# Hybrid decoder step: first loads and PSUM banks of the head rearranged, a tile for the extra tokens' values, decay rows spread by GpSimd

## Chip, cores and metric

The kernel runs on one core of a Trainium2 chip. The metric is the device time of one execution in microseconds; three runs of a kernel give a median. One further execution is recorded by the hardware profiler, and its trace is what the rows below come from.

## What is computed

One layer of a decoder over 2048 prompt tokens, 16 meta tokens in front of them, and 8 x 4 tokens of running requests ("extra tokens" are the 32 + 16). All read one input projection of the normalised stream (width 1024) and go through two groups of heads: four mLSTM heads, evaluated in chunks of 128 tokens, and a sliding-window attention. Both are gated, joined by one output projection, and normalised again. The mLSTM part, cut to what the change touches:

```python
b = jnp.cumsum(log_f, axis=1)                       # L tokens of a chunk, per head
dmat = b[:, :, None, :] - b[:, None, :, :] + log_i[:, None, :, :]     # causal, else -inf
inter = b + m[:, None, :]
m_t = jnp.maximum(inter, jnp.max(dmat, axis=2))     # running maximum
w = jnp.exp(dmat - m_t[:, :, None, :])
s_inter = jnp.exp(inter - m_t)
qk = einsum(q, k) * w
num = einsum(qk, v) + einsum(q, c) * s_inter[..., None]
w_state = jnp.exp(b_last[:, None, :] - b + log_i - m_new[:, None, :])
c_new = decay[..., None, None] * c + einsum(w_state, k, v)
```

The carried state starts from the meta tokens' chunk, so the first chunk of prompt tokens needs the meta tokens' gates, keys and values first.

## The kernel before

**Stages.** Prompt tokens go in 16 blocks of 128, a block being a chunk of the mLSTM part. A head prepares the weights: each projection's 1024 x 512 fp32 block is loaded in four parts (`load`), its maximum is taken, and it is split into two fp16 parts (`prep`, L271 on ScalarE and L274 on VectorE). Block 0 is projected with the fp32 weights as they arrive (L415), the later blocks and the extra tokens with the split ones (`proj`, L296 to L299; `proj_e`, L305 and L306). The first phase then runs through the chunks: four projections each (q, k, v, o), gates, the mLSTM steps, and the normalisation of a block two ahead (`norm_x`), with single steps of the extra tokens' work and of the later weights between. The second phase does the attention and output projections. The head lasts to 109.4 us here, the first phase to about 545 us.

**Order.** Instructions are placed on each engine's queue by a scheduler which works from the written order and its own model of times; each engine then takes its queue in order. The first loads are chained (`first`) so that SP issues them one behind the other. Rows of one chunk can stand among those of another.

**Tiles.** PSUM has four kinds of tile: `pj` (2 banks, projections), `pt` (3), `px` (1, extra tokens) and `po` (2). `xs` (two buffers) takes the token blocks as loaded: block 0 `x0`, the extra tokens `xe`, block 1 `x1`. `all_max` spreads a column's maximum to all partitions with a matmul of ones (L135) into a `pt` tile.

**A chunk's decay rows.** `m_rows` transposes the gate columns (L740, L741), scans them along the tokens, and leaves in partitions 0, 32, 64 and 96 one row for each head: `r2` (L748, L749) and `M` (L750). `m_weights` spreads the four rows of `M` to all 128 partitions by one fp32 matmul for each head with a selector `sel` (L759), which fills a `pt` tile `Mb`; from it come `ws` (L769), the weights `wt` (L773 and an exponential), and the inter-chunk factors `SI` (L775). `m_T` multiplies the queries by `SI` on GpSimd (L783, L784), `m_S` makes the weighted scores `At` (L794, L796), and `m_num` uses both (L807, L808). The extra tokens' `M5` is spread the same way (L656).

**Extra tokens.** `xe` is normalised, split and transposed to `ET`; its gates `ge` are a `proj_e` with the split gate weights, and its values `ve` lie in `vaug[1]`, the tile that odd chunks take for theirs (L428).

## Time and profile before

| | |
|---|---|
| time, median of 3 runs | 1077.33 us (1075.49 to 1078.78) |
| profiled execution, its own time | 1080.81 us |
| its span, first to last instruction | 1079.0 us |
| TensorE busy | 1035.4 us, 96% of the span |
| VectorE / ScalarE / GpSimd busy | 730.5 / 442.6 / 254.0 us |
| mean granted TensorE clock | 0.984 |
| moved by DMA | 161.83 MB, 150 GB/s |

Busy times are sums over an engine's instructions. A wait is the idle time in front of an instruction, put down to the event that ended it. Start times in the timelines count from the first instruction; matmuls overlap, so what one costs the queue is read from one start to the next.

### The profile page before, as it was taken

To read this page: it belongs to the slowest core of one execution; us is meant where nothing else is said; L and a number is where in the kernel's file an instruction comes from. 1 tells how busy PE (TensorE), PEld (TensorE's weight loads), DVE (VectorE), ACT (ScalarE), POOL (GpSimd) and SP (SyncE) were. 2 spreads that over 40 slices of the span, in tenths; PEclk is the share of its full clock that TensorE was granted. 3 is DMA by queue.
4 is the path that set the end of the run, shared out by engine and by line. 5 is a ranking of instruction groups with operands and counts; after the bars stand their busy time and mean duration, and the time that the engine had idled before them with its cause. 6 is when DMAs were issued, how large, how long until landed. Compare 5 with 4: busy or idle time off the path is not lost.

```text
span 1079.0 us, 17626 instructions
## 1 busy us (share of the span) xinstructions
PE 1035.4 (96%) x6391; PEld 573.5 (53%) x6391; DVE 730.5 (68%) x2057; ACT 442.6 (41%) x1112; POOL 254.0 (24%) x270
## 2 busy tenths in 40 slices
PE   6979998999999998998999999999999999999996
PEld 3435565655555554555564554555555555555553
DVE  5769666776867796877546686566666566666674
ACT  5646332244444445462234343433343433343430
POOL 2112231321120001113011141333322333322322
PEclk9998999999999998999999999999999999999998
DMA  9756447345785686655686455546445645545452
GB/s 323 202 141 164 110 120 173 97 126 145 232 235 143 190 239 168 208 132 145 232 265 112 79 131 127 137 119 126 102 123 125 132 115 131 110 110 131 113 122 63
DMA packets 245809, 161.83 MB, mean 150 GB/s; under 512 B 207945, under 2 KB 220953, under 8 KB 244409
## 3 DMA queue, kind: packets, MB, share of 16 engines
q1 hardware_dynamic: 245722, 160.70, 57.3%
q8 instruction: 50, 0.82, 0.3%
q14 instruction: 37, 0.30, 0.1%
HBM read 68.22 MB, written 43.58 MB: 104 GB/s over the span
## 4 chain that ended last, share of the span: by engine, by line
PE 65%; DMA 12%; DVE 11%; issue 5%; ACT 4%; POOL 1%; SPq 1%; DVEq 0%; ACTq 0%; POOLq 0%
PE pj L1341 15%; PE pj L299 13%; PE pj L296 12%; PE pj L297 12%; PE pt L1261 3%; DMA xT<-hl 2%; PE po L1314 2%; DMA ea<-in_dram 2%; DMA stg<-hl 1%; DMA kT<-kh 1%; DVE xs L380 1%; DMA wd_o<-w_o 1%; PE px L725 1%; ACT hl L323 1%; DMA da<-e_d 1%
## 5 line engine op out<-in xcount | busy, mean ns | idle before, releaser
L296 PEld LDWEIGHTS <-xT 128*128 128x128 f16 x992 | 98.0, 99 | 103.9 <-issue 7.5
L299 PEld LDWEIGHTS <-xT 128*128 128x128 f16 x992 | 97.0, 98 | 98.3 <-issue 2.9
L297 PEld LDWEIGHTS <-xT 128*128 128x128 f16 x992 | 98.0, 99 | 94.8 <-issue 4.3
L1341 PEld LDWEIGHTS <-EE 128*128 128x128 f16 x720 | 70.8, 98 | 80.3 <-issue 2.2
L1341 PE MATMUL pj<-w_o,EE 128*128 128x512 f16 x360 | 83.7, 384 | 0.0
L1341 PE MATMUL pj<-wr_o,EE 128*128 128x512 f16 x360 | 82.3, 379 | 0.0
L1268 ACT ACTIVATE SI<-SI,nb 128x272 f32<-128x272 f32 (+1 forms) x64 | 32.4, 507 | 66.1 <-DVE nb L1265 66.0
L325 POOL TENSOR_TENSOR lns<-lns,mhalf 128x1 f32<-128x1 f32 (+1 forms) x16 | 20.1, 1256 | 136.9 <-ACT lns L324 123.9
L296 PE MATMUL pj<-w_q,xT 128*128 128x512 f16 x120 | 46.4, 387 | 4.8 <-DMA xT<-hl 4.8
L1274 POOL TENSOR_TENSOR mhl<-SI,mhl 128x32 f16<-128x32 f32 x32 | 13.7, 430 | 157.3 <-ACT mhl L1273 157.3
L783 POOL TENSOR_TENSOR qs<-qT 128x512 f32<-128x512 f16 x16 | 23.2, 1453 | 113.5 <-DMA qT<-qh 50.1
L1268 ACT ACTIVATE g<-g,nb 128x272 f32<-128x272 f32 (+1 forms) x64 | 32.1, 503 | 42.7 <-DVE nb L1265 42.7
L296 PE MATMUL pj<-wr_z,xT 128*128 128x512 f16 x128 | 49.3, 385 | 0.0
L297 PE MATMUL pj<-wr_z,xT 128*128 128x512 f16 x128 | 49.2, 384 | 0.0
L296 PE MATMUL pj<-wr_az,xT 128*128 128x512 f16 x128 | 48.5, 379 | 0.0
L296 PE MATMUL pj<-wr_aq,xT 128*128 128x512 f16 x128 | 48.5, 379 | 0.0
L297 PE MATMUL pj<-wr_aq,xT 128*128 128x512 f16 x128 | 48.5, 379 | 0.0
L297 PE MATMUL pj<-wr_az,xT 128*128 128x512 f16 x128 | 48.5, 379 | 0.0
L296 PE MATMUL pj<-w_o,xT 128*128 128x512 f16 x120 | 47.3, 394 | 0.0
L297 PE MATMUL pj<-w_o,xT 128*128 128x512 f16 x120 | 47.1, 393 | 0.0
L1171 POOL TENSOR_TENSOR xs<-xs,gb 128x1024 f32<-128x1024 f32 (+1 forms) x16 | 42.8, 2675 | 15.4 <-DMA stg<-hl 9.3
L296 PE MATMUL pj<-w_v,xT 128*128 128x512 f16 x120 | 46.4, 386 | 0.0
(459 smaller groups left out, 2506.1 us busy)
## 6 DMA issues: line engine op xcount, KB each, us to landing
stg<-in_dram SPq DMA_DIRECT2D x28, 512.0 KB
xs<-in_dram SPq DMA_DIRECT2D x16, 512.0 KB
h_d<-xs SPq DMA_DIRECT2D x16, 512.0 KB
xT_d<-xT SPq DMA_DIRECT2D x16, 512.0 KB
xs<-h_d SPq DMA_DIRECT2D x16, 512.0 KB
xT<-xT_d SPq DMA_DIRECT2D x16, 512.0 KB
out_dram<-xs SPq DMA_DIRECT2D x15, 512.0 KB
hn_d<-g SPq DMA_DIRECT2D x16, 258.0 KB
```

The source lines that it names most:

```text
L296: T.matmul(ps, xT[:, k, :], w.t[:, k, 0, :n], start=(k == 0), stop=False)
L297: T.matmul(ps, xT[:, k, :], w.t[:, k, 1, :n], start=False, stop=False)
L299: T.matmul(ps, xT[:, KT + k, :], w.t[:, k, 0, :n], start=False, stop=(k == KT - 1))
L323: A.activation(junk[:, D:2 * D], x, AF.Square, bias=nmu, accum_out=ss)
L325: G.tensor_tensor(rs, ve, mhalf[:rows, 0:1], op=ALU.pow)
L783: G.tensor_tensor(c.qs, c.qT[:, 0], c.qT[:, 1], op=ALU.add)
L1171: G.tensor_tensor(z, z, lg[:rows], op=ALU.mult)
L1261: T.matmul(ps[:, lo:], c.qT[:, h], kTs[:, 2 * (h // 4) + x, lo:], start=(x == 0), stop=(x == 1))
L1268: A.activation(p[:, i, lo:], p[:, i, lo:], AF.Exp, bias=nb[:, h:h + 1], accum_out=sums[:, h:h + 1])
L1274: G.tensor_tensor(m[:, 1], p[:, :, 2 * P:], m[:, 0], op=ALU.subtract)
L1314: T.matmul(pso[:, h], l, r, start=False, stop=(i == len(last) - 1), skip_group_check=True)
L1341: T.matmul(ps, c.yT[:, a, :], w[:, k, t, :], start=(first and j == 0), stop=(last and j == len(mm) - 1))
```

## The change

There are five edits. The selector matmuls are replaced by GpSimd `partition_broadcast` instructions into an SBUF tile `Mb` (in `m_rows`, so that they are written right behind `M`) and, for `M5`, straight into `Mb5`; `sel` and its memsets go; the GpSimd library that is loaded is another one. The extra tokens' gates are computed in fp32 from eight transposes of `xe` and the unsplit gate weights, and that part of the code with its scans stands ahead of block 0's split. The gate weights, their bias and the constants are loaded ahead of w_k, and block 1 ahead of w_v. Before the chunks run, `all_max` and the first gates take `po` tiles. `ve` is a tile of the arena.

```diff
     def all_max(a, m):
         n = m.shape[1]
-        ps = pt([P, n, P])
+        ps = (pt if Order.running else po)([P, n, P])
...
-    G.load_library(library_config.standard)
+    G.load_library(library_config.all_libraries[10])
...
     first(xe, x_e)
-    stk = stage(512, "w")
-    load(stk, w_a[1])
-    bA = [bias_tile(0, 512, first), bias_tile(512, 512, first)]
     tg = cst.tile([P, KT, 8], F32, name="tg")
     first(tg, w_g)
     bg = cst.tile([P, 8], F32, name="bg")
     first(bg, b_in[0:1, 2560:2568].partition_broadcast(P))
+    first(cs[:, P:], consts[:, P:])
+    stk = stage(512, "w")
+    load(stk, w_a[1])
+    bA = [bias_tile(0, 512, first), bias_tile(512, 512, first)]
...
-    sel = cst.tile([P, H, P], F32, name="sel")
-    G.memset(sel, 0.0)
-    for h in range(H):
-        G.memset(sel[32 * h:32 * h + 1, h], 1.0)
...
         if n == 0:
-            ps = pt([P, 8])
+            ps = po([P, 8])
             proj32(ps, lambda k: tg[:, k])
...
-    ve = vaug[1][:NE]
+    ve = ea.take(H * 129).rearrange("p (h d) -> p h d", d=129)[:NE]
+    G.memset(ve[:, :, 128:129], 1.0)
...
     scale_qk(0)
+    x1 = work("xs", [P, D])
+    first(x1, x_p[P:2 * P, :])
     stv = stage(512)
     load(stv, w_a[2])
...
     dmat(ET, EE[:, 0])
-    first(cs[:, P:], consts[:, P:])
+    xef = work("kw", [P, 512])[:, 0:8 * NE].rearrange("p (k t) -> p k t", t=NE)
+    ps = pt([P, 8, NE])
+    for j in range(8):
+        T.transpose(ps[:, j], xe[:, j * P:(j + 1) * P], ident[:NE, :NE])
+    A.activation(xef, ps, AF.Copy)
+    ps = pt([P, 8])
+    for k in range(KT):
+        T.matmul(ps[:NE], xef[:, k], tg[:, k], start=(k == 0), stop=(k == KT - 1))
+    V.tensor_tensor(ge, ps[:NE], bg[:NE], op=ALU.add)
     log_sigmoid_rows(ge, NE, 1)
...
-    last = proj_e(ge, ET, wg, 8, bg, t1, ps=pt)
...
         Mb5 = ea.take(160).rearrange("p (h b s) -> p h b s", h=H, s=5)
-        ps = pt([P, H, 40])
         for h in range(H):
-            T.matmul(ps[:, h], sel[:, h], M5, start=True, stop=True)
-        A.activation(Mb5.rearrange("p h b s -> p (h b s)"), ps.rearrange("p h t -> p (h t)"), AF.Copy)
+            G.partition_broadcast(Mb5[:, h].rearrange("p b s -> p (b s)"), M5[32 * h:32 * h + 1], channels=P)
...
         V.scalar_tensor_tensor(M, r2[:, 1], carry.m, b, op0=ALU.subtract, op1=ALU.subtract)
-        c.r2, c.M = r2, M
+        Mb = work("Mb", [P, H, P])
+        for h in range(H):
+            G.partition_broadcast(Mb[:, h], M[32 * h:32 * h + 1], channels=P)
+        c.r2, c.Mb = r2, Mb
...
-        Mb = pt([P, H, P])
-        for h in range(H):
-            T.matmul(Mb[:, h], sel[:, h], c.M, start=True, stop=True)
+        Mb = c.Mb
...
     extra = jobs()
+    Order.running = True
```

The block from `xT0 = work(...)` to `a_proj(0, 1, stk)`, with block 0's split, its q and k projections and the splits of the gate weights and of w_k, is the same text and now stands behind the extra tokens' scans (behind `V.tensor_copy(tok, ...)`).

The scheduler orders all queues anew. Three places, with the new kernel's own line numbers in its rows. First SP in the head: `stg` are the staging tiles of w_q and then w_v, `stage` those of w_k and w_o, `xs` the token blocks, `EE` the extra tokens' split. Before:

```order
L114 DMA tg<-in_dram 128x64
L114 DMA bg<-in_dram 128x8
L114 DMA stage<-in_dram 128x1024 x4
L114 DMA bias<-in_dram 128x512
L101 DMA h_d_149<-xs 128x1024
L101 DMA_TRANSPOSE xT<-hl 128x16x128
L101 DMA_TRANSPOSE EE<-EE 128x8x128
L114 DMA stg<-in_dram 128x1024 x4
L114 DMA bias<-in_dram 128x512
L114 DMA cs<-in_dram 128x752
L114 DMA xs<-in_dram 128x1024
```

Now:

```order
L115 DMA cs<-in_dram 128x752
L115 DMA stage<-in_dram 128x1024 x4
L115 DMA bias<-in_dram 128x512 x2
L115 DMA stage<-in_dram 128x1024 x4
L115 DMA bias<-in_dram 128x512
L102 DMA ea<-in_dram 128x8
L102 DMA h_d_144<-xs 128x1024
L102 DMA_TRANSPOSE xT<-hl 128x16x128
L115 DMA xs<-in_dram 128x1024
L102 DMA_TRANSPOSE EE<-EE 128x8x128
L115 DMA stg<-in_dram 128x1024 x4
L115 DMA bias<-in_dram 128x512
```

The load of block 1 (`xs`, 128x1024) stood behind the loads of w_v, their bias and the constants, and now stands right behind the transpose of block 0.

Second, GpSimd where the chunks begin: L325 (now L324) is the `pow` of a block's normalisation, L783 and L784 (now L789 and L790) the two query operations, L716 (now L721) a step of the extra tokens, ISA the broadcasts. Before:

```order
L1027 MEMSET EE 128x1024
L783 TENSOR_TENSOR qs<-qT 128x512
L325 TENSOR_TENSOR lns<-lns,mhalf 128x1 x3
L673 MEMSET da 128x288
L674 MEMSET da 32x1
L784 TENSOR_TENSOR qs<-qs,SI 128x512
L783 TENSOR_TENSOR qs<-qT 128x512
L716 TENSOR_TENSOR da<-ea,cs 32x1024
```

Now:

```order
L324 TENSOR_TENSOR lns<-lns,mhalf 128x1
L789 TENSOR_TENSOR qs<-qT 128x512
L324 TENSOR_TENSOR lns<-lns,mhalf 128x1 x2
L678 MEMSET da 128x288
L679 MEMSET da 32x1
L662 ISA ea<-ea 128x40 x4
L758 ISA Mb<-rM 128x128 x4
L790 TENSOR_TENSOR qs<-qs,SI 128x512
L721 TENSOR_TENSOR da<-ea,cs 32x1024
L789 TENSOR_TENSOR qs<-qT 128x512
L324 TENSOR_TENSOR lns<-lns,mhalf 128x1
L758 ISA Mb<-rM 128x128 x4
```

A chunk's four broadcasts stand behind a `pow` and ahead of the product with `SI`; block 1's `pow` now comes ahead of the first query addition.

Third, VectorE around chunk 0's rows: `r` and `rM` are `r2` and `M` (L749, L750; now L754, L755), `w_o` the split of w_o, `xs` and `hl` block 3's normalisation and split, `vaug` and `px` the values of the extra tokens and of chunk 1. Before:

```order
L274 SCALAR_TENSOR_TENSOR w_o<-stage,cols,w_o 128x2x512
L749 SCALAR_TENSOR_TENSOR r_712<-fi,cols,rb 128x128
L750 SCALAR_TENSOR_TENSOR rM<-r_712,cols,rb 128x128
L274 SCALAR_TENSOR_TENSOR w_o<-stage,cols,w_o 128x2x512 x3
L379 SCALAR_TENSOR_TENSOR xs<-xs,lns,gb 128x1024
L309 TENSOR_TENSOR g<-g,bias 48x512
L380 SCALAR_TENSOR_TENSOR xs<-xs,lns,gb 128x1024
L315 SCALAR_TENSOR_TENSOR vaug_124<-px,cols,g 48x4x128
L769 TENSOR_TENSOR ws<-am,pt 128x4
L773 SCALAR_TENSOR_TENSOR wt<-pt,am,cs 128x128 x4
```

Now:

```order
L600 TENSOR_TENSOR ea<-ea 128x40
L602 COPY ea<-ea 128x32
L395 SCALAR_TENSOR_TENSOR hl<-xs,cols,hl 128x1024
L308 TENSOR_TENSOR g<-g,bias 48x512
L752 SCALAR_TENSOR_TENSOR rb<-ones,fi 128x128
L753 SCALAR_TENSOR_TENSOR r_708<-fi,cols 128x128
L603 TENSOR_TENSOR ea<-ea 128x32
L665 TENSOR_TENSOR ea<-ea 128x32 x4
L314 SCALAR_TENSOR_TENSOR ea<-px,cols,g 48x4x128
L754 SCALAR_TENSOR_TENSOR r_708<-fi,cols,rb 128x128
L427 SCALAR_TENSOR_TENSOR vaug_119<-pj,cols,bias 128x4x128
L755 SCALAR_TENSOR_TENSOR rM<-r_708,cols,rb 128x128
```

The split of w_o, the passes over block 3 and the extra tokens' values, which followed `M`, now stand ahead of it, and so does chunk 1's evacuation (L427), which came well behind `M` before.

## Rows read from the trace of the kernel before

**Rows 1.** Busy times by stage: stretch, length, each engine (instructions), clock, DMA share, GB/s.

```profile
0.00:109.40 109.40, 90.68 (x367) 45.18 (x368) 82.62 (x219) 63.63 (x114) 20.27 (x31) 0.95 0.72 207
109.40:545.00 435.60, 423.67 (x2623) 245.81 (x2622) 311.03 (x896) 179.65 (x405) 75.95 (x63) 0.98 0.61 171
545.00:1079.00 534.00, 521.03 (x3404) 282.49 (x3401) 336.88 (x944) 199.37 (x593) 157.81 (x177) 0.99 0.52 121
```

**Rows 2.** Timeline of TensorE, block 1: start, length, engine, line, operation, tiles [idle before].

```profile
64.47 0.61 PE L296 MATMUL pj<-w_q,xT 128*128 128x512 f16 x1 [4.84 <-DMA xT<-hl]
...
67.43 0.38 PE L297 MATMUL pj<-w_q,xT 128*128 128x512 f16 x1
```

**Rows 3.** Waits of TensorE over the span: who, for whom, total us, times, longest.

```profile
PE pt L740 <- DVE Gf L481: 4.0, 2, 3.3
...
PE px L305 <- ACT w_v L271: 2.7, 1, 2.7
```

**Rows 4.** Timeline of TensorE, chunk 0 (first two rows) and a later chunk.

```profile
92.53 0.98 PE L656 MATMUL pt<-ea,sel 128*128 128x40 f32 x8
93.34 0.39 PE L299 MATMUL pj<-w_v,xT 128*128 128x512 f16 x1
...
434.54 1.05 PE L759 MATMUL pt<-rM,sel 128*128 128x128 f32 x8
435.43 0.38 PE L762 MATMUL pt<-cs,r 128*128 128x128 f32 x2
...
445.58 0.39 PE L807 MATMUL po<-vaug,At 128*128 128x129 f32 x2
```

**Rows 5.** Groups of GpSimd by shape: tiles, shapes, count | busy us, mean ns | idle before.

```profile
L1171 POOL TENSOR_TENSOR xs<-xs,gb 128x1024 f32<-128x1024 f32 x15 | 40.5, 2697 | 13.9 <-DMA stg<-hl 9.3 <-DVE xs L1170 4.6
...
L843 POOL TENSOR_TENSOR kd<-kvu,kd 128x128 f16<-128x128 f32 x32 | 18.5, 598 | 17.8 <-ACT kd L841 10.9 <-issue 6.9
...
L218 POOL MEMSET Gf<- 128x128 f32 x2 | 0.4, 204 | 0.0
```

**Rows 6.** Timelines of VectorE and GpSimd in one chunk, in order of time.

```profile
419.98 0.15 DVE L475 TENSOR_TENSOR ls<-ls 128x4 f32<-128x4 f32 x1
...
420.57 1.15 POOL L783 TENSOR_TENSOR qs<-qT 128x512 f32<-128x512 f16 x1 [2.65 <-DVE ls L475]
...
420.88 0.87 DVE L476 TENSOR_SCALAR ls<-ls 128x4 f32<-128x4 f32 x1
...
430.47 0.34 DVE L750 SCALAR_TENSOR_TENSOR rM<-r,r,rb 128x128 f32<-128x128 f32 x1
...
434.85 1.32 POOL L325 TENSOR_TENSOR lns<-lns,mhalf 128x1 f32<-128x1 f32 x1 [13.13 <-ACT lns L324]
...
441.93 0.74 DVE L796 SCALAR_TENSOR_TENSOR At<-pt,cols,wt 128x512 f32<-128x512 f32 x1
```

**Rows 7.** Timeline of TensorE, transposes of the extra tokens' gate columns.

```profile
70.98 0.26 PE L581 MATMUL pt<-cs,Gf 48*128 48x48 f32 x1
71.08 0.22 PE L582 MATMUL pt<-cs,Gi 48*128 48x48 f32 x1
```

**Rows 8.** Groups of TensorE by shape in the first 109.4 us.

```profile
L415 PE MATMUL pt<-tg,SI 128*128 128x8 f32 x8 | 1.0, 256 | 0.0
```

**Rows 9.** Timelines of TensorE, VectorE, SP and ScalarE in the head, in order of time.

```profile
5.95 3.75 PE L367 MATMUL pj<-gbr,ones 1*128 1x512 f32 x4 [5.95 <-DVE mv_a L334]
...
18.17 1.28 DVE L371 SCALAR_TENSOR_TENSOR xs<-xs,rs_a,gb 128x1024 f32<-128x1024 f32 x1
...
35.29 0.68 SPq L114 DMA_DIRECT2D xs<-in_dram  x1
...
44.05 1.06 ACT L321 ACTIVATE hl<-xs 128x1024 bf16<-128x1024 f32 x1 [1.32 <-DMA xs<-in_dram]
...
88.05 0.35 DVE L750 SCALAR_TENSOR_TENSOR rM<-r,cols,rb 128x128 f32<-128x128 f32 x1
...
101.59 0.73 DVE L428 SCALAR_TENSOR_TENSOR vaug<-pj,cols,bias 128x512 f32<-128x512 f32 x1
```

More of the change, by code (lines that the diff above doesn't have):

```diff
@@ L95, in tile_hymba_step @@
         last = None
+        running = False
         anchor = None
@@ L558, in tile_hymba_step @@
     dmat(ET, EE[:, 0])
-    first(cs[:, P:], consts[:, P:])
-    xT0 = work("xT", [P, 2 * KT, P], F16)
-    A.activation(hl[:, 0], x0, AF.Copy, scale=s_x)
-    V.scalar_tensor_tensor(hl[:, 1], x0, s_x, hl[:, 0], op0=ALU.mult, op1=ALU.subtract)
-    dmat(xT0, hl.rearrange("p c d -> p (c d)"))
-    dma(h_d[0], x0)
-    x1 = work("xs", [P, D])
-    first(x1, x_p[P:2 * P, :])
-    Order.anchor = Order.last
-    a_proj(0, 0, stq)
-    wg = prep("g", [tg[:, 2 * i:2 * i + 2, :] for i in range(4)], 8)
-    a_gate(0)
-    last = proj_e(qe, ET, wA[0], 512, bA[0], t1)
-    dma(e_d[:, 0], qe)
-    wA[1] = prep("k", stk, 512, sums=(0,2))
-    scale_qk(1)
-    sc_qk = col()
-    V.tensor_scalar(sc_qk, i_qk[1], QSC, None, op0=ALU.mult)
-    a_proj(0, 1, stk)
-    last = proj_e(ge, ET, wg, 8, bg, t1, ps=pt)
+    xef = work("kw", [P, 512])[:, 0:8 * NE].rearrange("p (k t) -> p k t", t=NE)
[7 more added lines that the diff above has]
+    V.tensor_tensor(ge, ps[:NE], bg[:NE], op=ALU.add)
     log_sigmoid_rows(ge, NE, 1)
@@ L621, in tile_hymba_step @@
     V.tensor_copy(tok, ptr[:NE, :, 0:P:32])
+    xT0 = work("xT", [P, 2 * KT, P], F16)
+    A.activation(hl[:, 0], x0, AF.Copy, scale=s_x)
+    V.scalar_tensor_tensor(hl[:, 1], x0, s_x, hl[:, 0], op0=ALU.mult, op1=ALU.subtract)
+    dmat(xT0, hl.rearrange("p c d -> p (c d)"))
+    dma(h_d[0], x0)
+    Order.anchor = Order.last
+    a_proj(0, 0, stq)
+    wg = prep("g", [tg[:, 2 * i:2 * i + 2, :] for i in range(4)], 8)
+    a_gate(0)
+    last = proj_e(qe, ET, wA[0], 512, bA[0], t1)
+    dma(e_d[:, 0], qe)
+    wA[1] = prep("k", stk, 512, sums=(0,2))
+    scale_qk(1)
+    sc_qk = col()
+    V.tensor_scalar(sc_qk, i_qk[1], QSC, None, op0=ALU.mult)
+    a_proj(0, 1, stk)
     dma(xT_d[0], xT0)
```

## Prediction

> **What bounds the kernel now.** I read the busy times by stage first, then TensorE's waits, then single stretches. The cuts are where chunk 2's first projection begins (109.4 us) and where the second phase's projections begin (545 us). In the middle stage TensorE is busy for 423.67 of 435.60 us and VectorE for 311.03; in the last one TensorE for 521.03 of 534.00 [rows 1]. So in these two every microsecond taken off TensorE's queue counts, as long as the others keep pace. The head is another matter: TensorE is busy for 90.68 of 109.40 us there and VectorE for 82.62 [rows 1], and what ends last changes from step to step. TensorE stands 4.84 us for the second token block's transposed activations [rows 2] and 2.7 us for the split of w_v [rows 3]; the projection behind the first of these starts slowly, its first seven matmuls at 0.61 to 0.63 us where later ones record 0.38 [rows 2]. In the middle stage the longest waits are for the gate rows, 4.0 us in all [rows 3].
>
> **Part 1, decay rows by GpSimd.** A chunk's four selector matmuls (eight records) go. They hold TensorE from 434.54 to 435.43, 0.89 us [rows 4]. Fifteen of the sixteen chunks have theirs in the middle stage: 15 x 0.89 = 13.4 us off a queue with 12 us of idle time in 436, so I count all of it. The first chunk's, and the extra tokens' like it (92.53 to 93.34, 0.81 us [rows 4]), lie in the head, 1.7 us, and are counted there.
>
> GpSimd gets four broadcasts of 128x128 a chunk, which this trace does not show. From below, a memset of that shape records 204 ns; from above, the nearest instruction that reads and writes 128x128 is a subtraction at 598 ns [rows 5]. I take 0.4 us, the middle, since a broadcast reads one row but writes all: 1.6 us a chunk, 0.8 to 2.4. GpSimd is busy for 75.95 of 435.6 us in this stage [rows 1], so 16 x 1.6 = 26 us more don't make it a bound. What matters is when the spread rows reach their readers. In the chunk at 430 us the row was ready at 430.81 (430.47 plus 0.34), TensorE took it up only at 434.54, the weighted scores were done at 442.67 (441.93 plus 0.74) and TensorE used them at 445.58 [rows 4, 6]. So there are 3.7 us of queue ahead of the old spreading and 2.9 us behind its last consumer. In the new order the broadcasts can stand behind the `pow` of a layer norm, as in that chunk, where it started at 434.85 and took 1.32 [rows 6]: 436.2 + 1.6 = 437.8, against 435.43 by matmul. That is 2.4 us later, inside the 2.9. Price of the move on the critical path: nothing, with 0.5 us to spare in this chunk. The bank of PSUM that the spread rows held is free for other work; I count nothing for that.
>
> The trace shows what GpSimd work can do to VectorE: a 128x4 operation of 0.15 us recorded 0.87 us at 420.88, when GpSimd was in its 1.15 us addition from 420.57 [rows 6]. The Trainium skill, "GPSIMD Engine Reference" (section 8, Key points), has the rule that speaks against this part: GpSimd shares its SBUF interfaces with VectorE, with contention for VectorE instructions in a two-port mode or with two SBUF inputs. The trace agrees, with the 0.87 us. If each chunk's broadcasts stretched VectorE by all of 2.4 us, it would have 15 x 2.4 = 36 us more, 347 of some 422 us: not yet the bound, so the sum stays, but the second rival below has its chance from it.
>
> **Part 2, the extra tokens' gates in fp32.** Sixteen small fp16 matmuls go (about 0.4 us together); eight transposes of 48 columns and eight fp32 matmuls of 8 columns come. Two transposes of that kind start 0.10 us apart, so about 1 us [rows 7]; eight records of the fp32 kind add up to 1.0 us, and there are sixteen, so at most 2.0, and half of it if they overlap as much as others [rows 8]. Net 1.6 to 2.6 us more on TensorE, in the stretch of fp32 projections, where no wait of [rows 2, 3] falls: it counts there. In return the gates no longer wait for the split of the gate weights.
>
> **Part 3, first loads.** The load of token block 1 was issued at 35.29, behind the four loads of w_v, which wait for the staging tiles; its first reader started at 44.05 after a DMA wait [rows 9]. In the new order it stands right behind block 0's transpose, which needs block 0 (below: 15.5 us), the extra tokens' first pass ahead of it on VectorE and its own split of 1.28 us. I choose 27 to 28 for the issue and, as no load of w_v is ahead of it any more, 31 for the landing. Normalising and splitting it takes 3 x 1.28 us on VectorE among other work, so that its transpose is ready near 51 instead of 64.4. TensorE reaches this projection when it has finished the fp32 ones, at 59.63 before (64.47 less 4.84). So the wait of 4.84 us goes, with the slow start: seven matmuls in 2.96 us, where 0.38/0.63 of that is 1.8, so 1.2 us. Together 6.0 us. The two constants moved ahead of the w_k load (0.4 MB) delay it by a microsecond or two, hidden as w_k's readers come later.
>
> **Part 4, PSUM banks of the head.** The bias row's two matmuls now go first and the reductions use the `po` banks. Block 0 was ready at 19.45 (18.17 plus 1.28 [rows 9]); its last step reads the bias row. TensorE's first pair of such matmuls began at 5.95 and took 3.75 us [rows 9]; two pairs in a row, bias first, end at 13.4, and a half pass of 0.7 and the last step of 1.28 make 15.5. The copies that follow on ScalarE come behind the w_q sums, so TensorE's first projection moves up by about 3 us rather than 4, and part 2's 1.6 to 2.6 us come off that: 1 us is left.
>
> **Part 5, `ve` apart.** Chunk 1's values were taken out of PSUM only at 101.59 [rows 9], since they share a tile with the extra tokens' values, which had first to be used and stored; the next projection waited for the bank. In the new VectorE order this comes ahead of chunk 0's row M. VectorE is then what ends last in the head: M was ready at 88.40 (88.05 plus 0.35 [rows 9]), and I put the new M at about 87.5, hardly earlier, but with 9 to 10 us of VectorE work done before it that came after it in the old order (block 3's three passes at 1.28, three quarters of the w_o split at 1.28 each, four passes of the kind at 101.59, 0.73).
>
> **Sum.** Head: 6 (part 3), 1 (parts 4 and 2), 1.7 (first chunk's spreading), and 2 to 3 of the wait for w_v and the late bank (part 5) make about 11; by VectorE's work before M it is 9 to 10. I take 10. Middle: 13.4. Last stage: nothing changes, 0. So 23.4 us off the profiled execution's 1080.8, which is 1057.4. That execution is 3.5 us above the median of 1077.3, so the forecast for the median is 1054. Ends: the head between 4 (VectorE's order absorbs most) and 14, the middle between 8 and 16 (its 12 us of idle time can grow or shrink with a new order): 12 to 30 off, 1047 to 1065.
>
> **Rivals.** First, the head gives next to nothing: VectorE's queue, not the transfers, sets each start. For it: M is hardly earlier. Against it: the 4.84 us wait ends with a DMA. Then 13.4 plus about 1: 1063. Second, the middle gives half back: VectorE stretched by GpSimd brings the gate rows late, the wait of 4.0 us in [rows 3], and a few more of it: half of 13.4 is 6.7, 0.45 us a chunk: 1061. Third, the library that is asked for at the start is not resident, and its loading holds the first `pow` on GpSimd, which block 0 needs at about 14.5 us; a hold beyond that costs one for one, up to some 5 us: 1059. Fourth, on the other side: GpSimd as the gate of every chunk. It decides from the point where four broadcasts outlast the 3.7 + 2.9 us of room; each microsecond beyond costs 15 us, so above 2.05 us a broadcast (8.2 less 6.6 is 1.6, times 15 is 24) the whole gain is gone. At 2.7 us each, the mean of GpSimd's 128x1024 products [rows 5], it is 10.8 less 6.6, 4.2 x 15 = 63, less 24: 39 over 1077, so 1116, slower. Against it: nothing of 128x128 comes near 2 us.
>
> **How the numbers follow.** Chances: forecast 0.62; head gives nothing 0.13; half given back in the middle 0.13; library 0.05; GpSimd as gate 0.05; 0.02 for no change. The range 1045 to 1066 holds the first four cases, less their tails, about 8 in 10. About 0.3% (3 us) is what a measurement of this kernel tells from no change: faster 0.92, same 0.03, slower 0.05.
>
> **What would show it.** Right: in the middle stage some 13 us less between chunk 2's first projection and the second phase; that projection begins near 99 us instead of 109.4; block 1's projection begins near 58 with no DMA wait ahead; a broadcast records 0.2 to 0.6 us; the last stage still takes 534 us. Wrong: TensorE waits for weighted scores or gated queries once a chunk; GpSimd's first `pow` comes after 14 us; the middle stage shortens by less than 8 us with VectorE late at the gate rows.

## Result: 1066 us, 12 to 14 us less than before; the forecast was 23 us less

| | before | after |
|---|---|---|
| time, median | 1078.05 us (1075.49 to 1083.71, 4 runs) | 1065.99 us (1064.34 to 1067.51, 4 runs) |
| ratio, 95% interval | | 0.987 [0.984, 0.990] |
| profiled execution, its own time / span | 1080.81 / 1079.0 us | 1064.34 / 1062.4 us |
| TensorE busy | 1035.4 us | 1017.7 us |

By the ratio the change is 1.3% faster (1.0 to 1.6%), about 14 us; the two medians lie 12 us apart, and the profiled executions 16.5. The busy time of the kernel after by stage, cut at chunk 2's first projection and at the second phase (start:end, length, busy time and count of each engine, granted TensorE clock, DMA share, GB/s):

```profile
0.00:94.10 94.10, 84.43 (x344) 41.76 (x345) 75.66 (x209) 62.86 (x112) 16.49 (x34) 0.98 0.80 237
94.10:528.20 434.10, 412.58 (x2517) 231.76 (x2516) 318.13 (x904) 181.54 (x407) 102.81 (x124) 0.99 0.62 170
528.20:1062.40 534.20, 520.73 (x3405) 281.80 (x3403) 342.53 (x944) 200.27 (x593) 158.87 (x176) 0.99 0.53 123
```

Beside [rows 1], with the second phase taken from where it starts there, 544.7, the head has lost 15.3 us (109.4 to 94.1), the middle stage 1 us (435.3 to 434.1), the last stage nothing (534.3 to 534.2). The cut is not quite fair: chunk 0's numerators, 16 records that held TensorE from 102.45 to 104.24 before, 1.8 us, stood in the head and now stand behind it. Put back, the head has lost 13.5 and the middle 3. In the middle TensorE is busy for 10.8 us less, 12.6 with those numerators put back, near the 13.4 that the selector matmuls promised, and idle for 21.5 us where it was idle for 11.9. What it waits for there (what waited, what ended the wait, us in all, times, longest):

```profile
PE pt L745 <- DVE Gf L480: 8.5, 3, 4.7
PE pt L768 <- DVE r L754: 3.5, 2, 1.9
PE px L730 <- DVE ea L714: 1.9, 1, 1.9
PE po L813 <- DVE cols L126: 1.2, 1, 1.2
PE po L829 <- DVE sm L968: 1.2, 1, 1.2
```

The 4.0 us for the gate rows [rows 3] have become 8.5, and the transposes of the rows `r`, which never waited before, now do. So much of the freed TensorE time shows up as waiting, most of it for VectorE's rows. The broadcasts themselves (duration min/median/max in ns, first and last start):

```profile
L758 POOL PARTITION_BROADCAST Mb<-rM x64: 422/427/1509, 82.5 to 515.0; - x64
```

The head, from the timeline (start, duration, engine, line, what it writes from what; in brackets the idle time ahead of it):

```profile
16.09 1.97 PE L447 MATMUL pt<-cs,xs 128*128 128x128 f32 x8 [0.40 <-DVE xs L370]
...
19.46 1.06 PE L414 MATMUL pj<-stg,wt 128*128 128x512 f32 x1
...
27.89 0.37 SPq L115 DMA_DIRECT2D xs<-in_dram  x1
...
58.94 0.38 PE L295 MATMUL pj<-w_q,xT 128*128 128x512 f16 x1
...
81.42 0.74 DVE L427 SCALAR_TENSOR_TENSOR vaug<-pj,cols,bias 128x512 f32<-128x512 f32 x1
82.08 0.33 DVE L755 SCALAR_TENSOR_TENSOR rM<-r,cols,rb 128x128 f32<-128x128 f32 x1
...
82.50 1.33 POOL L758 PARTITION_BROADCAST Mb<-rM  x4 [2.15 <-DVE rM L755]
```

Block 1's load is issued at 27.89 instead of 35.29 [rows 9], and its first projection starts at 58.94 with no wait and at 0.38 us a matmul, where it started at 64.47 behind 4.84 us of waiting [rows 2]. Chunk 1's values leave PSUM at 81.42 instead of 101.59, ahead of M, which is ready at 82.4 instead of 88.4 [rows 9]. Four broadcasts follow M within 0.1 us and take 1.33.

### The profile page after: what moved, and what is told of

The parts are those of the page before. It is cut to its first block, busy times and chain, and to the rows that moved or that the text cites. A ratio compares the mean times of both kernels' runs of the same rounds, so it can differ in the third digit from the quotient of the medians.

```text
span 1062.4 us, 17449 instructions
## 1 busy us (share of the span) xinstructions
PE 1017.7 (96%) x6263; PEld 555.3 (52%) x6263; DVE 736.3 (69%) x2056; ACT 444.7 (42%) x1111; POOL 278.2 (26%) x334
## 4 chain that ended last, share of the span: by engine, by line
PE 56%; DVE 15%; DMA 13%; ACT 6%; issue 5%; POOL 2%; SPq 1%; DVEq 0%; POOLq 0%; ACTq 0%
PE pj L1348 13%; PE pj L295 11%; PE pj L296 11%; PE pj L298 11%; DMA xT<-hl 4%; PE pt L1268 2%; PE po L1321 2%; DMA stg<-hl 2%; DVE xs L379 1%; SPq L104 1%; DVE hl L1277 1%; DMA stg<-in_dram 1%; DMA At<-hn_d 1%; DMA da<-e_d 1%; DMA wd_o<-w_o 1%
## 5 line engine op out<-in xcount | busy, mean ns | idle before, releaser
L296 PEld LDWEIGHTS <-xT 128*128 128x128 f16 x992 | 97.2, 98 | 94.1 <-issue 1.5
L1348 PE MATMUL pj<-wr_o,EE 128*128 128x512 f16 x360 | 87.3, 379 | 0.2 <-DMA EE<-stg 0.2
L758 POOL PARTITION_BROADCAST Mb<-rM x64 | 24.7, 485 | 115.1 <-DVE rM L755 114.2
L1281 POOL TENSOR_TENSOR mhl<-g,mhl 128x32 f16<-128x32 f32 x32 | 18.9, 589 | 135.9 <-ACT mhl L1280 135.9
L1277 DVE TENSOR_TENSOR hl<-g,hl 128x512 f16<-128x512 f32 (+1 forms) x32 | 24.6, 768 | 40.8 <-ACT hl L1276 40.8
L1281 POOL TENSOR_TENSOR mhl<-SI,mhl 128x32 f16<-128x32 f32 x32 | 18.1, 566 | 123.7 <-ACT mhl L1280 118.8
L296 PE MATMUL pj<-w_q,xT 128*128 128x512 f16 x120 | 45.7, 381 | 0.0
L295 PE MATMUL pj<-w_q,xT 128*128 128x512 f16 x120 | 45.7, 381 | 0.0
```

Of the source, the lines that this page charges most:

```text
L295: T.matmul(ps, xT[:, k, :], w.t[:, k, 0, :n], start=(k == 0), stop=False)
L296: T.matmul(ps, xT[:, k, :], w.t[:, k, 1, :n], start=False, stop=False)
L758: G.partition_broadcast(Mb[:, h], M[32 * h:32 * h + 1], channels=P)
L1277: V.tensor_tensor(hl[:, 1, 2 * q:2 * q + 2, lo:], p[:, :, lo:2 * P], hl[:, 0, 2 * q:2 * q + 2, lo:], op=ALU.subtract)
L1281: G.tensor_tensor(m[:, 1], p[:, :, 2 * P:], m[:, 0], op=ALU.subtract)
L1348: T.matmul(ps, c.yT[:, a, :], w[:, k, t, :], start=(first and j == 0), stop=(last and j == len(mm) - 1))
```

## Experiments

Theory A is the prediction's: TensorE's queue sets the middle stage, so each microsecond taken off it counts. Theory B, from the trace after: what is taken off comes back as waits for VectorE's rows. Theory C: the difference lies in the order that the scheduler makes for a given combination of parts. Others are named where they come up.

All runs in one view first. The middle stage is cut as above, by the profiled execution of each; "end" is where the second phase starts, in us from the first instruction; "clock" is the granted TensorE clock, the mean over all runs of a kernel.

| kernel | spreading | ratio to before, 95% | end | middle | TensorE busy | idle | clock |
|---|---|---|---|---|---|---|---|
| before | matmul | 1 | 544.7 | 435.3 | 423.4 | 11.9 | 0.988 |
| e3_neutral | matmul | 0.9987 [0.9965, 1.0009] | 543.2 | 432.7 | 417.5 | 15.2 | 0.989 |
| e6_x1 | matmul | 0.9951 [0.9927, 0.9975] | 541.3 | 428.1 | 418.8 | 9.3 | 0.989 |
| e2_head | matmul | 0.9925 [0.9900, 0.9951] | 535.5 | 438.7 | 424.2 | 14.5 | 0.991 |
| e10_less | matmul, o cut | 0.9937 [0.9891, 0.9983] | 534.7 | 423.5 | 409.3 | 14.2 | 0.987 |
| e14_dead | GpSimd, dead matmuls | 0.9881 [0.9854, 0.9908] | 533.3 | 437.6 | 423.8 | 13.8 | 0.994 |
| after | GpSimd | 0.9871 [0.9839, 0.9903] | 528.2 | 434.1 | 412.6 | 21.5 | 0.989 |
| e4_twice | GpSimd, twice | 0.9854 [0.9791, 0.9917] | 537.3 | 441.0 | 416.4 | 24.6 | 0.990 |
| e1_spread | GpSimd, old head | 1.0047 [1.0023, 1.0071] | 551.2 | 437.2 | 412.1 | 25.1 | 0.983 |
| e5_free | none | 0.9932 [0.9909, 0.9955] | 539.7 | 442.6 | 416.8 | 25.8 | 0.989 |
| e9_free_old | none, old head | 1.0042 [1.0024, 1.0060] | 549.3 | 434.9 | 411.9 | 23.0 | 0.983 |
| e11_sinks | GpSimd | 0.9862 [0.9830, 0.9893] | 527.3 | 433.4 | 412.8 | 20.6 | 0.990 |
| e12_both | GpSimd | 0.9821 [0.9787, 0.9854] | 527.1 | 429.4 | 411.5 | 17.9 | 0.991 |
| e13_kz | GpSimd | 0.9830 [0.9800, 0.9861] | 525.4 | 430.9 | 412.8 | 18.1 | 0.993 |

Where chunk 2 starts moves with each order, so "end" compares better than "middle"; the idle column is what to read first. With the four matmuls a chunk on TensorE it reads 9 to 15 us, without them 18 to 26, on either head and whether GpSimd spreads, spreads twice or nobody does.

The waits are not all of it: TensorE's clock goes with them. In the kernel after, TensorE stood for 4.75 us until 493.70, and the clock was at the lower of its two levels (1.2 and 2.4 GHz) from 491.9 on, until 498.7 (columns as in the stages):

```profile
485.00:491.80 6.80, 3.95 (x23) 2.03 (x21) 6.70 (x8) 0.00 (x0) 5.80 (x3) 1.00 0.21 40
491.90:498.60 6.70, 4.90 (x15) 2.88 (x16) 5.13 (x21) 1.10 (x2) 1.29 (x4) 0.50 0.44 98
```

At that level a projection matmul starts 0.42 us behind the one before it, at the higher level 0.21 (rows of e1_spread below). So one minus the clock, times the span, is an estimate of the most that the clock can have cost: about 13 us before, 12 after, 18.7 in e1_spread, 6.6 in e14_dead. No run separates the clock from the waits.

**e1_spread: part 1 alone**

```diff
 # kernel before
-        c.r2, c.M = r2, M
+        Mb = work("Mb", [P, H, P])
+        for h in range(H):
+            G.partition_broadcast(Mb[:, h], M[32 * h:32 * h + 1], channels=P)
+        c.r2, c.Mb = r2, Mb
 # m_weights, Mb5, sel and the library as in the change
```

> The kernel before with part 1 alone: the decay rows (and the extra tokens' M5) spread by GpSimd broadcasts, the selector and its matmuls gone; first loads, gates, PSUM banks and the tile of ve as before. Theory A, the prediction's: TensorE's queue sets the middle stage, so 15 x 0.89 = 13.4 us go there and 1.7 us in the head: about 1063 where the kernel before takes 1078, middle stage near 422 us with no more than 13 us of TensorE idle time in it. Theory B, read from the changed kernel's trace: the middle gives most of it back, since TensorE then stands for VectorE's gate rows: 1072 to 1075, middle stage near 431 us with some 20 us of idle time. Theory C: the giving back comes from the meeting of the new head and the new middle, not from the broadcasts: then this kernel, with the old head, comes out like A.

1087.65 us: slower than before, by 0.5%, which none of the theories had. The middle has B's idle time (25.1), and the head lost ground too. One chain in it, from the timeline:

```profile
88.17 0.34 DVE L744 SCALAR_TENSOR_TENSOR rM<-r,cols,rb 128x128 f32<-128x128 f32 x1
88.43 3.67 DVE L270 SCALAR_TENSOR_TENSOR w_o<-stage,cols,w_o 128x1024 f16<-128x1024 f32 x3
92.02 1.27 DVE L375 SCALAR_TENSOR_TENSOR xs<-xs,lns,gb 128x1024 f32<-128x1024 f32 x1
...
88.59 5.89 POOL L747 PARTITION_BROADCAST Mb<-rM  x4 [12.40 <-DVE rM L744]
...
94.52 0.63 ACT L770 ACTIVATE SI<-Mb 128x512 f32<-128x512 f32 x1 [4.54 <-POOL Mb L747]
...
95.36 0.68 ACT L304 ACTIVATE g<-px,cols 48x512 f32<-48x512 f32 x1
...
100.30 2.06 PE L638 MATMUL po<-vaug,kw 16*128 16x129 f32 x8 [7.29 <-DVE da L681]
...
102.69 0.64 PE L302 MATMUL px<-w_o,EE 128*128 128x512 f16 x1
103.11 0.63 PE L301 MATMUL px<-w_o,EE 128*128 128x512 f16 x1
...
105.28 0.38 PE L301 MATMUL px<-w_o,EE 128*128 128x512 f16 x1
105.49 0.38 PE L302 MATMUL px<-w_o,EE 128*128 128x512 f16 x1
```

Four broadcasts took 5.89 us beside VectorE's passes over w_o and block 3, which kept their own 1.22 to 1.27 us each. ScalarE stood 4.54 us for them with the extra tokens' values (`g`) queued behind, and TensorE 7.29 us for what is made of those; that wait was 1.43 us before. The matmuls behind it run at the lower clock until 104.8, as the stretch shows (clock 0.50):

```profile
98.10:104.80 6.70, 4.50 (x14) 2.67 (x15) 5.92 (x14) 3.85 (x10) 0.00 (x0) 0.50 0.55 154
```

Over all runs the clock was 0.983 here and 0.988 in the runs of the kernel before that were made beside these: by the estimate above 18.7 against 13.3 us, 5.4 of difference, as much as the kernel lost.

**e2_head: all but part 1**

```diff
 # kernel after: sel, its matmuls and the standard library back
+        Mb = pt([P, H, P])
+        for h in range(H):
+            T.matmul(Mb[:, h], sel[:, h], c.M, start=True, stop=True)
-        Mb = c.Mb
```

> The changed kernel with part 1 undone: the spreading is done by selector matmuls again (library and selector tile as before), the other four edits stay. Theory A: the head is worth 10 us, the middle stage takes the 435 us it had: 1068, about 2 to 3 us slower than the changed kernel only because part 1's size was smaller than said. Theory B: the head is worth 12 us or more by itself, and the broadcasts 2 to 5: 1068 to 1071. Theory C: the new head disturbs the middle even without the broadcasts: idle time of TensorE in the middle stage above 18 us, where the kernel before has 12; then 1072 or more.

1073.42 us, 0.75% or 8 us faster than before. The idle time of the middle is 14.5 us, so the new head does not disturb it (C falls in this form). Part 1 on this head is then worth the step from 0.9925 to 0.9871, some 6 us (1 to 10 by the two intervals), where it was forecast at 15.

**e3_neutral: another order of ScalarE and VectorE**

```diff
 # kernel before, m_weights
-        A.activation(c.em, am[:, 1], AF.Exp, scale=-1.0)
-        A.activation(c.em, c.em, AF.Copy, scale=s_qk[0])
 ...
         A.activation(c.dec, c.SI[:, :, P - 1], AF.Copy)
+        A.activation(c.em, am[:, 1], AF.Exp, scale=-1.0)
+        A.activation(c.em, c.em, AF.Copy, scale=s_qk[0])
```

> The kernel before with two ScalarE steps of each chunk (the exponential of em and its scaling) written behind the factors SI instead of ahead of the weights. TensorE's queue keeps its order word for word; 138 rows of ScalarE's and 32 of VectorE's move. It leaves nothing out and removes no work, so it shows what a mere reordering of the two off-path engines is worth. Theories A and B: within 2 us of the kernel before (1076 to 1080), so that differences of 5 us in the other runs mean something. Theory C: 3 us or more either way, as waits depend on small shifts.

1079.34 against 1080.47: no difference, as A and B had it. TensorE's own order is unchanged, and these shifts of the others did not matter. Its profiled execution also shows what single executions are worth: with the same TensorE queue the middle stage is 2.6 us shorter than before and idle for 3.3 us more, at a clock of 1.00 there instead of 0.98.

**e4_twice: the broadcasts doubled**

```diff
 # kernel after
         for h in range(H):
             G.partition_broadcast(Mb[:, h], M[32 * h:32 * h + 1], channels=P)
+        for h in range(H):
+            G.partition_broadcast(Mb[:, h], M[32 * h:32 * h + 1], channels=P)
```

> The changed kernel with each chunk's four broadcasts issued twice, the second time into the same place with the same data: readers wait for the second, so the spread rows come some 1.9 us later (4 x 0.48) and GpSimd has 31 us more to do over the 16 chunks. Theory A (2.9 us of slack behind the last reader) and theory B (VectorE's gate rows, made before the broadcasts, are the late ones): within 4 us of the changed kernel, 1064 to 1070. The rival that GpSimd's broadcasts hold each chunk: 15 x 1.9 = 29 us more, 1095. If broadcasts stretched VectorE's operations as GpSimd's products do, VectorE would be busy for some 30 us more.

1066.69 us, like the change itself (1058.89 to 1072.39, so less sharp than the others, some 7 us either way). The rival by which GpSimd gates each chunk, here 29 us, is out. VectorE's busy time in the middle rose from 318.1 to 326.7 us, far from 30.

**e5_free and e9_free_old: nobody spreads**

```diff
 # kernel after (e5_free), kernel of e1_spread (e9_free_old)
+    MB0 = work("Mb", [P, H, P])
+    V.memset(MB0, 0.0)
 ...
-        Mb = work("Mb", [P, H, P])
-        for h in range(H):
-            G.partition_broadcast(Mb[:, h], M[32 * h:32 * h + 1], channels=P)
-        c.r2, c.Mb = r2, Mb
+        c.r2, c.Mb = r2, MB0
```

> The changed kernel with the chunks' spreading left out altogether: no broadcast, no selector matmul; the readers of the spread rows take a tile that is cleared once, so the chunk's M is written and not read (its numbers are therefore wrong, the work after it is the same). What is left of the spreading is nothing, so this is the most that any way of spreading could bring. Theory B (TensorE's shorter queue runs into VectorE's late gate rows, whoever spreads): middle stage 428 to 434 us with 17 us of TensorE idle time or more, 1060 to 1066. Theory D (the broadcasts' own latency, 1.4 us and in some chunks 3 us, is what the middle pays with): middle stage near 424 us, idle time back to 12 us, 1055 to 1057.

> The kernel of part 1 alone, on the old head, with the chunks' spreading left out in the same way (the spread rows are a tile that is cleared once). Theory D (the broadcasts cost what part 1 alone lost; in the head the first chunk's four took 5.89 us and ScalarE stood for them): head back to 109 us, middle near 424 us, about 1065. Theory B: the head comes back to 109 us, since only there the broadcasts were long; the middle stays above 430 us with 17 us of idle time or more: 1073 to 1080.

1072.90 and 1084.15 us. Theory D, that the broadcasts' latency is what the middle pays with, falls twice: with no spreading at all the idle time stays at 25.8 and 23.0 us. On the new head the kernel with less to do is even 0.6% slower than the change; besides the broadcasts only the orders of the queues differ, so orders that the scheduler makes can lie some 7 us apart. On the old head the long wait shrank from 7.29 to 2.79 us, but the time stayed: the 5.89 us of broadcasts are not why part 1 alone loses. The lower clock is large enough to account for it: 0.983 in these runs too, as in e1_spread, against 0.988 before. Which of the order's waits go with it was not found.

**e10_less: the same TensorE time from another place**

```diff
 # kernel before
-    def proj(ps, xT, w, n):
+    def proj(ps, xT, w, n, low=KT):
 ...
-        for k in range(KT):
-            T.matmul(ps, xT[:, KT + k, :], w.t[:, k, 0, :n], start=False, stop=(k == KT - 1))
+        for k in range(low):
+            T.matmul(ps, xT[:, KT + k, :], w.t[:, k, 0, :n], start=False, stop=(k == low - 1))
 ...
-            proj(ps, c.xT, wA[i], 512)
+            proj(ps, c.xT, wA[i], 512, KT if i < 3 else 4)
```

> The kernel before, selector matmuls and all, with four of the 24 matmuls of each chunk's o projection left out (half of the low part of the activations times the high part of w_o; the output projection's input differs slightly). It takes 15 x 4 x 0.217 = 13.0 us off TensorE's queue in the middle stage and touches no other engine's work: the same size as the selector matmuls, from another place. Theory A: 13 us less, 1067. Theory B: the waits for VectorE take back more than half: 1072 to 1077, middle stage 429 us or more, idle time 18 us or more.

1073.38 us, in B's range, but not in B's way. The stages two and three (the same columns as above):

```profile
111.20:534.70 423.50, 409.28 (x2578) 239.34 (x2577) 310.77 (x897) 177.29 (x400) 76.19 (x62) 1.00 0.63 175
534.70:1072.60 537.90, 522.46 (x3395) 282.72 (x3392) 336.31 (x947) 201.18 (x600) 158.70 (x177) 0.99 0.53 122
```

The middle stage is 11.8 us shorter than before, its idle time only 2.3 us longer; that idle time is no longer than e3_neutral's, so B's "any shorter queue runs into VectorE" does not show here. But the clock of the stage was 1.00 in this execution and 0.98 before [rows 1], which by the estimate above can be 5 of the 11.8 us. The head, where only chunk 1's four matmuls go, and the last stage, which the edit does not touch, were 1.8 and 3.6 us longer. Over all runs, at the clock of the kernel before, the 13 us brought 6.8 (2 to 12 by the interval): some of it counted, and not all. Whether these matmuls count for more than the selector matmuls is not shown: the intervals of this run and of e14_dead (below) leave room for both to be alike.

**e6_x1: block 1's load alone**

```diff
 # kernel before
     scale_qk(0)
+    x1 = work("xs", [P, D])
+    first(x1, x_p[P:2 * P, :])
     stv = stage(512)
 ...
-    x1 = work("xs", [P, D])
-    first(x1, x_p[P:2 * P, :])
```

> The kernel before with one part of the first loads alone: token block 1's load stands ahead of w_v's instead of behind it. Theory A (prediction, part 3): block 1's first projection no longer waits for its transposed activations (4.8 us) and starts fast (1.2 us): it begins near 59 us; 1074 if all six stay. If VectorE or the split of w_v sets the head further on, the gain is taken back by chunk 2's first projection (109.4 us): 1079 or more.

1075.06 against 1080.14: 5 of the 6 us stay. Block 1's first projection starts at 61.12 without a wait. A new wait of 5.1 us (for the extra tokens' transposes) appears in the head, yet the end keeps the gain.

**e11_sinks, e12_both, e13_kz: single blockers taken away**

```profile
485.38 2.35 POOL L1178 TENSOR_TENSOR xs<-xs,gb 32x1024 f32<-32x1024 f32 x1 [0.91 <-DVE ls L472]
487.80 2.34 POOL L1179 TENSOR_TENSOR xs<-xs,gb 32x1024 f32<-32x1024 f32 x1
490.11 1.14 POOL L789 TENSOR_TENSOR qs<-qT 128x512 f32<-128x512 f16 x1
...
485.23 0.16 DVE L472 RECIPROCAL ls<-ls 128x4 f32<-128x4 f32 x1
485.42 2.33 DVE L473 TENSOR_TENSOR ls<-ls 128x4 f32<-128x4 f32 x1
487.78 0.16 DVE L474 TENSOR_TENSOR ls<-ls 128x4 f32<-128x4 f32 x1
487.98 2.20 DVE L475 TENSOR_SCALAR ls<-ls 128x4 f32<-128x4 f32 x1
490.21 1.07 DVE L477 SCALAR_TENSOR_TENSOR ls<-ls 128x4 f32<-128x4 f32 x1
...
493.70 0.44 PE L745 MATMUL pt<-cs,Gf 128*128 128x128 f32 x1 [4.75 <-DVE Gf L480]
```

These rows of the change's timeline show its longest wait in the making: three operations on 128x4 last as long as GpSimd's products beside them.

```diff
 # kernel after: e11_sinks
+    sink_t = col(AH)
+    dma(sink_t, sinks.partition_broadcast(P))
     for n in range(NCH + 1):
 # e12_both: that, and in final()
-        G.tensor_tensor(z, z, lg[:rows], op=ALU.mult)
-        G.tensor_tensor(z, z, lb[:rows], op=ALU.add)
+        e = G if rows == P else V
+        e.tensor_tensor(z, z, lg[:rows], op=ALU.mult)
+        e.tensor_tensor(z, z, lb[:rows], op=ALU.add)
 # e13_kz: both, and in d_head()
-        G.tensor_tensor(kz, ...
+        V.tensor_tensor(kz, ...
```

> The changed kernel with one load moved: the eight sinks of the second phase are loaded before the chunks begin, where they stood behind the chunks' code and their load was issued in chunk 11 at 408.3 us; VectorE's next instruction then stood 3.74 us for it at 412.3, ahead of that chunk's scans, and TensorE 1.61 us for the rows r. TensorE's order stays the same. Theory E (the gate chain is late because VectorE and ScalarE stand behind single slow instructions that the order did not expect): the wait for r in chunk 11 goes, middle stage 1.5 to 3 us shorter, 1063 to 1065 where the changed kernel takes 1066. Theory C (waits move about with any reordering): the 1.6 us come back at another place.

> The same, and the two products of the extra tokens' last normalisation (32x1024, 2.35 us each on GpSimd) done by VectorE. In the changed kernel they ran from 485.38 to 490.14, and three small operations of chunk 14's gate rows, 0.16 us each elsewhere, recorded 2.33, 2.20 and 1.07 us beside them and GpSimd's next product; TensorE then stood 4.75 us for these gate rows. Theory E: no operation of the gate rows is held there any more, that wait falls below 1.5 us, and with the sinks' load it makes 4 to 6 us: 1060 to 1062. Theory C: middle stage idle time stays at 20 us or more, 1064 to 1068.

> The same as the last, and the extra tokens' four products kz (32x1024, 2.19 us each on GpSimd) done by VectorE too; the first of them held one operation of chunk 2's gate rows for 2.78 us, where TensorE stood 2.92 us. Theory E: that wait goes as well, 2 to 3 us more: 1058 to 1060. Against it: VectorE has some 4 us more work of its own in the same stretches, which can make other rows late; then 1061 to 1064.

1065.35, 1061.55 and 1062.47 us. In the first, the wait for `r` in chunk 11 is gone and one of 3.57 us stands five microseconds later, where 0.34 stood: theory C. In the second the wait of 4.75 us is gone, as E said, and so is more than half of the gate rows' total; new ones are 3.0 us for `At`, 2.8 for `dg` and 3.5 for `am`. The waits of its middle stage:

```profile
PE pt L510 <- ACT am L770: 3.5, 2, 3.3
PE pt L745 <- DVE Gf L480: 3.1, 2, 1.9
PE po L813 <- DVE At L802: 3.0, 1, 3.0
PE pt L136 <- DVE dg L135: 2.8, 1, 2.8
```

Its second phase starts at 527.1, with e11_sinks at 527.3. e12_both is the fastest kernel here (0.982), but its interval reaches into that of the change, so a gain over it is likely rather than shown. e13_kz adds nothing.

**e14_dead: the matmuls back, as dead work**

```diff
 # kernel after, m_weights; c.M kept
         Mb = c.Mb
+        idle = pt([P, H, P])
+        for h in range(H):
+            T.matmul(idle[:, h], ident, c.M, start=True, stop=True)
```

> The changed kernel with four fp32 matmuls of 128x128 a chunk put back on TensorE as dead work: same input M, same count, form and place as the selector matmuls, their result read by nobody and their PSUM tile free as soon as they end, while the spread rows still come from GpSimd. They cost TensorE's queue the 13.4 us that part 1 took off in the middle stage. Theory F (half of what part 1 took off TensorE stood where TensorE would otherwise wait, since it reaches the gate and state rows that much sooner): idle time of the middle stage falls from 21.5 to 12 to 15 us, as in the five kernels with selector matmuls; the stage grows by 4 to 7 us only; 1070 to 1074. Theory G (it is not TensorE's queue but the PSUM tile that is no longer held through the weights, or the other order of the queues): idle time stays above 19 us and the whole 13 us come on top: 1077 to 1081.

1067.04 us: 1 us above the change (an estimate from the two intervals: 1 us with some 4.5 either way), less than even F expected. Its stages:

```profile
0.00:95.70 95.70, 83.97 (x351) 42.34 (x352) 76.27 (x209) 62.45 (x111) 16.68 (x34) 1.00 0.79 234
95.70:533.30 437.60, 423.77 (x2637) 245.34 (x2637) 322.16 (x904) 182.36 (x407) 105.82 (x124) 1.00 0.61 169
533.30:1065.00 531.70, 519.66 (x3405) 282.00 (x3403) 336.23 (x944) 198.99 (x593) 156.98 (x176) 0.99 0.52 123
```

and the waits of its middle stage that answer to those of the change:

```profile
PE pt L745 <- DVE Gf L480: 5.5, 3, 3.5
PE pt L768 <- DVE rM L755: 1.2, 2, 0.7
PE px L705 <- DVE ea L700: 1.1, 1, 1.1
```

TensorE is busy for 11.2 us more in the middle and idle for 7.7 us less, so the stage is 3.5 us longer. The second phase starts 5.1 us later, 1.6 of which stand in the head, where TensorE's first matmul came at 7.89 for 6.31; the last stage, which the dead work does not touch, is 2.5 us shorter here. The clock helped: it was 0.991 to 0.996 in these five runs and 0.987 to 0.990 in the four of the change, by the estimate above 6.6 against 12.0 us. So the 13 us that part 1 took off TensorE's queue had cost little there, 1 us and by the intervals at most 5.5: put back, they fill 7.7 us of waiting in this execution, and up to 5.4 us more come back with the clock.

G falls as it was put: the idle time does not stay and the 13 us do not come on top. But this kernel has e2_head's matmuls on TensorE and is some 5 us faster than it (0.9881 and 0.9925; 1 to 9 us by the intervals). So, by the medians, most of the 6 us that part 1 brings on this head do not come from TensorE's queue. The PSUM tile that is no longer held through the weights, the rows spread sooner and the other order are left for them, and no run tells these apart.

## Why the prediction was right in direction, and the gain it forecast 9 to 11 us too large

**What bounds the kernel: the step that failed.** "In these two every microsecond taken off TensorE's queue counts" was read from a busy share of 97%. For the selector matmuls it did not hold: 13 us of the same matmuls, put back, cost 1 us (e14_dead). For the o projection's matmuls it held in part: 13 us taken off brought 6.8 (e10_less). The condition in that sentence, that the others keep pace, is where it broke: the waits for the gate rows and for the rows `r`, 8.5 and 3.5 us in the kernel after, are 5.5 and 1.2 with the dead matmuls put back. The clock is a term that the sum left out: by the estimate above it can have taken back up to 5.4 us of what the shorter queue gave.

**Part 1, size right, worth wrong.** TensorE's busy time fell as worked out: 12.6 us in the middle with the 1.8 that moved in put back. Counting all of it as gain was the mis-sized term: forecast 13.4 in the middle and 1.7 in the head, measured some 6 (0.9925 to 0.9871), and of these only about 1 from TensorE's queue (e14_dead). The rest comes from what the prediction counted as nothing; the free PSUM bank may be part of it. The broadcast was put at 0.4 us and records 0.427; four take 1.33 in chunk 0 and 1.31 in most others. They were expected behind a `pow`, 2.4 us later than the matmuls; they begin 0.1 us behind M in 15 of the 16 chunks, so M is spread after 1.4 to 1.5 us in 13 of them (2.9 to 3.5 in the other three), where the chunk at 430 us needed 3.7 and 0.89 [rows 4, 6]. Their own price on the path was forecast at nothing; doubling them cost nothing that 7 us either way can tell (e4_twice).

**The Trainium skill's rule.** By the rows of e1_spread, broadcasts and VectorE do meet, but the other way round from what part 1 feared: VectorE's passes kept their 1.22 to 1.27 us, the four broadcasts went from 1.33 to 5.89. GpSimd's products do stretch VectorE: 0.16 us became 2.33. The Trainium skill, "GPSIMD Engine Reference" (section 8, Key points), has contention for the shared SBUF interfaces. Both rows agree with it. The 36 us that the prediction worked out as its worst case did not come: VectorE is busy for 7.2 us more in the middle (310.9 and 318.1).

**Parts 2 and 4.** Block 0 was ready just ahead of 16.09, where its transposes start after 0.40 us of waiting for it; 15.5 was forecast. The first projection moved from 21.69 to 19.46, 2.2 us for 3. The extra gates cost about 1.1 us net on TensorE (0.63 for the eight transposes, 0.81 for the matmuls, less the 0.36 of the old ones), for 1.6 to 2.6.

**Part 3.** Issue at 27.89 for 27 to 28, no wait and no slow start at 58.94 for about 58: right, and e6_x1 alone brought 5 of the 6 us.

**Part 5.** The mechanism was right, chunk 1's values leave PSUM 20 us sooner; that M is hardly earlier (87.5) was wrong: 82.4. That is where the head gained more than said, chunk 2 beginning at 94.1 for 99, 1.8 of the 5 us being work that moved behind the cut.

**Sum.** All but part 1 was worth 8 us (e2_head), for 8.3 (10 less the 1.7 of part 1); part 1 was worth 6, for 15.1; the last stage 0, as said. 1066 lies at the very end of the range that was given with the chances, 1045 to 1066, and 1 us outside the sum's own 1047 to 1065. That it is still inside owes something to luck.

**The rivals.** The second one, half of the middle given back with the gate rows late, is what came, and its place is right, 8.5 us of waits where 4.0 stood. Its mechanism is only half right: the idle time is there without broadcasts too (e5_free, e9_free_old), and the stretching of VectorE that shows comes from GpSimd's products, which the kernel before had as well. The prediction's own sign of being wrong, a middle stage shorter by less than 8 us with VectorE late at the gate rows, came too: 3 us. The library rival left no trace: the first `pow` starts at 6.3 us, and at 6.2 before. The GpSimd gate is out (e4_twice).

**Open.** Which link of the chunk's chain takes the place of TensorE was not isolated: each blocker that was removed let another wait appear (e11_sinks, e12_both). Part 1 alone, on the old head, loses 0.5%, which the lower clock can explain in size; which waits bring the clock down there, and not on the new head, stays open. So does what brings the 5 us of part 1 that do not come from TensorE's queue.

## What to carry to other kernels

A high busy share says that an engine has little idle time, not that each of its instructions costs time: here, matmuls that stood ahead of rows that TensorE would otherwise wait for were nearly free, and taking them away bought waits and a lower clock. Before an edit of that kind, put the same work back as dead instructions, or take the same time from another place of the queue; 13 us cost 1 in the first test and brought 7 in the second. Read the granted clock beside each time before a difference of some microseconds is given a cause. And where a scheduler orders all queues anew, measure the parts in combination: part 1 cost 5 us on one head and brought 6 on the other.

## What the runs showed of the hardware that was not expected

- VectorE and GpSimd hold each other, and either can be the one that waits: a 128x4 operation recorded 2.33 us beside a product of 2.35 on GpSimd, while four broadcasts took 5.89 us for 1.33 beside VectorE's passes of 1.22 to 1.27 over 128x1024. In both cases the one that had started first kept its own time (the product at 485.38 against 485.42, the pass at 88.43 against 88.59). The Trainium skill, "SBUF — State Buffer" (section "SBUF: two separate sides"), calls the pair of ports that the two share an exclusive lock, which whoever starts first keeps for its whole instruction. The rows agree: the operation that started at 485.42 ended with the product that had started at 485.38.
- The last stage, the same code in all of these kernels, took between 531 (e5_free: 1070.7 less 539.7) and 537.9 us (e10_less) in the profiled executions. The clock of that stage was 1.00 in the first and 0.99 in the second. Differences of 3 us between single executions say little.
- A wait of TensorE can be paid for twice. In e1_spread it stood 7.29 us until 100.30, the clock was at its lower level from 98.1 to 104.8, and the matmuls behind the wait came 0.42 us apart instead of 0.21.
